# Matmul spacing taken from the trace, in the build-time estimate that orders a two-block network's threads

## The chip, the cores and the metric

The kernel runs on one core of one Trainium2 chip. The metric is the device time of one execution in microseconds (us), the median of several runs.

## The reference, cut to what matters

Two blocks of two layers each, one after the other, in 32-bit floats; the width is 1024.

```
x = first_block(x, c, ctx, ...)          # 256 tokens x and 256 of context, depth 2
    per layer: x += 0.5 * gate * swiglu(norm(x) @ w1) @ w2
               x += gate * mixer(norm(x))     # layer 0 gated delta rule, layer 1 windowed attention
               x += 0.5 * gate * swiglu(norm(x) @ w1) @ w2
return second_block(x, positions, ...)   # 256 tokens, depth 2
    per layer: mix = (x @ w_in -> RG-LRU and latent attention, merged) @ w_out
               x = layer_norm(ALPHA * x + mix)
               ffn = (gelu(conv(x @ w_up)[gate]) * conv(x @ w_up)[value]) @ w_down
               x = layer_norm(ALPHA * x + ffn)
```

The gated delta rule of layer 0 has 8 heads. For each head and both directions it needs the inverses of unit lower triangular matrices of 128 (one for each of four chunks).

## The kernel before, in words

**Dense products.** Each weight piece (128 rows, 1024 or 768 columns) is loaded by SyncE into an `r` tile. `convert` (L464) rounds it to a high part with `copy` (a CAST from `r` to a `w` tile, on ScalarE or VectorE), and `lower` (L482) subtracts to get a low part with `flex` (a TENSOR_TENSOR from `r`, `w` to `w`, on VectorE or GpSimd). `mm3` (L518) then runs three matmuls for each 128 x 128 piece of weights: high with high, high with low, low with high. The moving side has 512 tokens in the first block and 256 in the second. Such matmuls read `p<-b,w` in the trace.

**Small fp32 products.** The mixers use plain 32-bit matmuls (`p<-b,b`); each of these leaves two records in the trace. In the delta rule each head goes through `dn_first` (L1062, grams and decays), `dn_solve` (L1175), `dn_join` (L1214), `dn_inverse` (L1313) and `dn_scan` (L1347). `dn_solve` sends the diagonal blocks of 32 to DRAM (`d<-b`) and back in another layout (`r<-d`), inverts their blocks of 16 in 28 small GpSimd instructions, each in place on the result of the one before, and sends the result back by DRAM (`d<-r`, `b<-d`). `dn_join` puts the blocks together, 16 to 32 to 64 to 128, in six groups of small matmuls (the first is `16*32 16x16`, then 32x16, 32x32, two of 64x64 and so on) with a VectorE or ScalarE step between each two.

**What sets the order.** Nothing is scheduled on the chip: each engine executes its instructions in the order in which the program was built. The build keeps one thread for the main products (priority 9) and spawns threads for everything else: the join has priority 1, the solve 2, grams and scan 3, the tiles of the projection 5. Every call on an engine first goes through `Ker.note` (L278), which adds an estimated duration to that engine's clock and remembers when each tile is written and read. `Ker.run` (L337) takes the first thread in rank whose data are ready when the TensorE clock gets there:

```
r = max([self.wrote[x.tensor.name][0] + 200 for x in aps], default=0.0)
if e:
    r = max(r, self.clock[e] - SLACK)
if best is None or r < best[0]:
    best = (r, th)
if r <= self.clock["tensor"]:
    break
```

The same clocks choose engines: `flex` (L402) takes VectorE or GpSimd, `copy` (L409) ScalarE or VectorE, `affine` (L416) ScalarE or VectorE, each the one that would be through first, counted from the later of its own clock and TensorE's. Their durations are formulas: a copy of n elements is 75 + 0.83 n ns on ScalarE and 65 + 0.52 n on VectorE, a subtraction 65 + 1.04 n on VectorE and 60 + 2.28 n on GpSimd.

In the second block `query_rope` (through `rope`, L1866) turns four tiles of queries per layer, each with one matmul of 256 columns against a constant `b` tile; the stage of w_up (48 pieces per layer, 24 matmuls of 256 columns each) is the longest dense stage. All instructions are issued from one helper, so every row of the trace names line L242 (after the change L260) and is told apart by its tiles: `w` weight parts, `r` raw weights, `b` blocks, `p` PSUM banks, `s` small tiles, `io` and `cbf` constants.

Of the kernel before, what the change touches and what calls it, by code (L numbers as in the profile page):

```python
# [8 lines left out]
F32 = mybir.dt.float32  # L9
F32R = mybir.dt.float32r  # L10
# [6 lines left out]
P = 128  # L17
# [10 lines left out]
# ---------------------------------------------------------------- constants and columns  # L28
# [68 lines left out]
def vec(a):  # L97
    """[..., 128*n] -> [128, prod(...)*n]: a column for each feature tile."""
    import numpy as np

    return np.ascontiguousarray(a.reshape(-1, P).T)
# [16 lines left out]
def pack_w(w):  # L118
    """[K, N] -> [N/128, 128, K]: for an output tile, partition p holds W[k*128+p, 128 columns] for each k."""
# [6 lines left out]
def layouts(a):  # L126
    """The device's arrays from the inputs: layout only."""
# [14 lines left out]
    # the first two slots with the summed features on the partitions, the others with the outputs there  # L142
# [12 lines left out]
    # six tiles of outputs: from the heads that are there early by two, for three tiles, and from each of the others  # L155
# [37 lines left out]
# ---------------------------------------------------------------- order of the work  # L193
# [4 lines left out]
def weave(items, extra):  # L198
    """extra spread evenly among all but the first and the last items, in order."""
# [9 lines left out]
def pieces():  # L209
    """The weights in the order in which they are used: what each product thread pulls next."""  # L210
# [19 lines left out]

class Engine:
    """An engine of the core: each instruction also goes on the estimate of when the engines are busy."""
# [24 lines left out]
class Ker:  # L257
# [19 lines left out]
    # -- the estimate of time, and the threads that it orders  # L277
    def note(self, eng, op, a, k):  # L278
# [7 lines left out]
        if eng == "tensor":  # L286
            if op == "matmul":
                m = aps[2]
                n = math.prod(m.shape[1:])
                c = n * {F32: 1.68, BF16: 0.44}.get(m.dtype, 0.422)  # L290
                if m.dtype == F32 and o.shape[0] <= 64:
                    c *= o.shape[0] / P
            else:
                c = 109.0
# [30 lines left out]
    def need(self, *aps, b=0, p=0, s=0, when=None, e=None):  # L325
        """What a thread waits for: data, free blocks, banks and small tiles, a condition, an engine."""
        return aps, b, p, s, when, e
# [9 lines left out]
    def run(self):  # L337
        """Steps of the threads: the first in rank that can go on when the tensor engine gets there."""
# [20 lines left out]
    # -- memory on chip  # L359
# [1910 lines left out]
```

## Time and profile before

| what | value |
|---|---|
| three runs | 2881.67, 2881.69 (median), 2883.3 us |
| span of the profiled execution | 2879.2 us |
| TensorE (PE) busy | 2760.1 us, 96% |
| VectorE (DVE) busy | 2161.7 us, 75% |
| ScalarE (ACT) busy | 909.9 us, 32% |
| GpSimd (POOL) busy | 672.1 us, 23% |
| chain that ended last | PE 82%, DVE 11%, issue 3%, ACT 2% |

The profiled execution's time is told by its span, 2879.2 us, which lies 2.5 us under the median of the runs; no other time of that execution is shown. The share of the chain says for how much of the span each engine did the work that the end waited for.

### The profile page before, as it was taken

The numbers are of one execution on the slowest core, as the hardware profiler recorded it, in microseconds if no ns is written. First come the engines' busy times: TensorE is split into PE (matmuls) and PEld (weight loads), VectorE is DVE, ScalarE is ACT, GpSimd is POOL, SyncE is SP. The second block draws the span as 40 slices with busy tenths as digits, with TensorE's granted clock in tenths as the row PEclk, the third lists the DMA queues.
The fourth block names the chain that finished last, engine by engine and source line by source line (L and its number), as shares of the span: only waits on it lengthen the run. The fifth ranks groups of instructions, "written<-read, shape, count | busy, mean of one in ns | idle before, by whom it ended". The sixth has DMA issues, their size and how long they took to land.

```text
span 2879.2 us, 47744 instructions
## 1 busy us (share of the span) xinstructions
PE 2760.1 (96%) x18916; PEld 2461.9 (86%) x18916; DVE 2161.7 (75%) x3981; ACT 909.9 (32%) x1979; POOL 672.1 (23%) x678
## 2 busy tenths in 40 slices
PE   7999999999989999999999999999898999999998
PEld 6888888888868888888888877999888998888998
DVE  4788878767766777758866587975878986878995
ACT  2111126435423111021111254214654333753432
POOL 2000234435412000120001322102413322512230
PEclk9999999989999999999999999999999999999999
DMA  6556542212122545535665312655434555334653
GB/s 242 193 181 196 190 162 74 55 43 60 38 96 89 187 151 178 159 109 195 193 202 176 110 62 80 190 179 172 140 110 146 183 176 164 127 110 129 197 174 118
DMA packets 145121, 412.59 MB, mean 143 GB/s; under 512 B 31233, under 2 KB 38145, under 8 KB 144897
## 3 DMA queue, kind: packets, MB, share of 16 engines
q1 hardware_dynamic: 144896, 409.54, 44.9%
q8 instruction: 149, 2.44, 0.4%
q14 instruction: 76, 0.61, 0.1%
HBM read 397.95 MB, written 11.53 MB: 142 GB/s over the span
## 4 chain that ended last, share of the span: by engine, by line
PE 82%; DVE 11%; issue 3%; ACT 2%; POOL 1%; DMA 1%; SPq 0%; POOLq 0%; ACTq 0%; DVEq 0%
PE p L242 82%; DVE b L242 7%; DVE w L242 3%; ACT b L242 2%; DVE s L242 1%; POOL b L242 1%; ACT w L242 1%; POOL w L242 0%; DMA b<-in_ada 0%; DMA b<-in_xt 0%; POOL s L242 0%; ACT L242 0%; DMA b<-d 0%; DVE gs L242 0%; DMA d<-r 0%
## 5 line engine op out<-in xcount | busy, mean ns | idle before, releaser
L242 PE MATMUL p<-b,w 128*128 128x256 f32 (+1 forms) x14166 | 2370.6, 328 | 36.2 <-ACT b L242 13.2
L242 PEld LDWEIGHTS p<-b,w 128*128 128x128 f32 x14166 | 2090.1, 193 | 256.3 <-ACT b L242 17.6
L242 DVE TENSOR_TENSOR w<-r,w 128x1024 fp32r<-128x1024 f32 (+1 forms) x512 | 653.8, 1280 | 54.0 <-ACT w L242 41.6
L242 POOL TENSOR_TENSOR b<-b,b 128x256 fp32r<-128x256 f32 (+3 forms) x262 | 274.6, 1060 | 748.8 <-ACT b L242 559.7
L242 POOL TENSOR_TENSOR w<-r,w 128x1024 fp32r<-128x1024 f32 (+1 forms) x79 | 190.8, 2415 | 1016.3 <-ACT w L242 868.3
L242 DVE CAST w<-r 128x1024 fp32r<-128x1024 f32 (+1 forms) x366 | 262.1, 716 | 184.9 <-PE p L242 153.0
L242 DVE SCALAR_TENSOR_TENSOR b<-r,b 128x512 f32<-128x512 f32 x448 | 343.7, 767 | 11.4
L242 ACT CAST b<-b 128x256 fp32r<-128x256 f32 (+1 forms) x284 | 130.7, 467 | 657.2 <-DVE b L242 571.3
L242 ACT CAST w<-r 128x1024 fp32r<-128x1024 f32 (+1 forms) x225 | 228.4, 1021 | 245.2 <-PE p L242 127.8
L242 PE MATMUL p<-b,b 128*128 128x128 f32 (+8 forms) x2872 | 272.5, 260 | 23.8 <-DVE b L242 15.3
L242 PEld LDWEIGHTS p<-b,b 32*32 32x32 f32 (+4 forms) x2872 | 213.5, 149 | 64.5 <-issue 20.9
L242 DVE TENSOR_TENSOR b<-b,b 128x256 fp32r<-128x256 f32 (+3 forms) x245 | 158.6, 653 | 117.1 <-ACT b L242 112.0
L242 ACT ACTIVATE b<-b 128x256 f32<-128x256 f32 (+1 forms) x188 | 90.8, 495 | 425.3 <-DVE b L242 404.8
L242 ACT ACTIVATE b<-p 128x128 f32<-128x128 f32 (+2 forms) x280 | 114.8, 415 | 293.0 <-PE p L242 292.7
L242 DVE TENSOR_TENSOR b<-b,p 128x256 f32<-128x256 f32 (+1 forms) x234 | 114.9, 501 | 45.7 <-PE p L242 39.5
L242 DVE SCALAR_TENSOR_TENSOR b<-p,par_t,b 128x255 f32<-128x255 f32 (+2 forms) x240 | 106.3, 474 | 16.0 <-ACT b L242 14.8
L242 ACT COPY b<-p 128x512 f32<-128x512 f32 (+5 forms) x161 | 71.7, 458 | 129.6 <-PE p L242 69.1
L242 PE MATMUL p<-io,b 128*128 128x128 f32 (+3 forms) x580 | 88.6, 281 | 19.4 <-DVE b L242 11.8
L242 POOL TENSOR_TENSOR b<-b 128x256 f32<-128x256 f32 x50 | 57.7, 1154 | 175.3 <-DVE b L242 175.3
L242 PEld LDWEIGHTS p<-io,b 128*128 128x128 f32 (+2 forms) x580 | 69.2, 163 | 33.6 <-DVE b L242 10.4
L242 DVE SCALAR_TENSOR_TENSOR b<-p,mod,b 128x256 f32<-128x256 f32 x92 | 40.7, 478 | 71.3 <-PE p L242 71.3
L242 POOL TENSOR_TENSOR s<-s,mhalf 128x4 f32<-128x4 f32 (+2 forms) x36 | 35.6, 990 | 182.5 <-DVE s L242 171.3
(105 smaller groups left out, 1324.1 us busy)
## 6 DMA issues: line engine op xcount, KB each, us to landing
r<-in_w SPq DMA_DIRECT2D x240, 512.0 KB, 3.7
r<-in_ada SPq DMA_DIRECT2D x128, 512.0 KB, 4.2
r<-in_w_up SPq DMA_DIRECT2D x96, 512.0 KB, 3.6
r<-in_w_in SPq DMA_DIRECT2D x76, 512.0 KB, 3.7
r<-in_w_down SPq DMA_DIRECT2D x48, 512.0 KB, 3.6
r<-in_dn_in SPq DMA_DIRECT2D x33, 512.0 KB, 3.6
r<-in_w SPq DMA_DIRECT2D x32, 384.0 KB, 3.3
b<-in_ada SPq DMA_DIRECT2D x32, 256.0 KB, 5.4
```

Of the source, the lines that this page charges most:

```text
L242: return fn(*a, **k)
```

## The change

In `note`, the cost of a TensorE instruction now comes from a function of the weights, the moving tile and the columns, with the numbers that the trace shows for the spacing of such matmuls. Removed comments and docstrings change nothing in the program.

```diff
+PARTS = {(32, 32): 28.0, (16, 32): 29.0, (64, 64): 57.0}
+
+def array_ns(w, x, cols):
+    n, rows = math.prod(x.shape[1:]), w.shape[0]
+    if x.dtype == BF16:
+        return 6.0 + n / 2.4
+    if x.dtype == F32R:
+        return max(112.0, 13.3 + n / 2.4)
+    if (rows, cols) in PARTS:
+        return 2 * PARTS[rows, cols]
+    part = (0.62 if rows <= 64 else 1.0) * (0.25 if cols <= 32 else 0.5 if cols <= 64 else 1.0)
+    return 2 * part * max(110.0, n / 1.2)
...
         if eng == "tensor":
-            if op == "matmul":
-                m = aps[2]
-                n = math.prod(m.shape[1:])
-                c = n * {F32: 1.68, BF16: 0.44}.get(m.dtype, 0.422)
-                if m.dtype == F32 and o.shape[0] <= 64:
-                    c *= o.shape[0] / P
-            else:
-                c = 109.0
+            c = array_ns(aps[1], aps[2], o.shape[0]) if op == "matmul" else 112.0
```

The set of TensorE instructions is the same. In the estimate a dense matmul of 512 columns goes from 216 to 226.6 ns, one of 256 from 108 to 120.0 ns, a block of 32 x 32 from 13.4 to 56 ns, one of 16 columns on 32 rows from 6.7 to 58 (16 rows) or 56 ns, one of 64 x 64 from 53.8 to 114 ns. Over the program the choice of engine moves, from before to after: CAST of 1024 columns to `w` on VectorE 340 to 388, on ScalarE 199 to 151; CAST of 768 columns on VectorE 26 to 30, on ScalarE 26 to 22; low parts of 1024 columns on VectorE 472 to 483, on GpSimd 67 to 56; low parts of 768 on VectorE 40 to 42, on GpSimd 12 to 10; TENSOR_TENSOR `b<-b` of 256 columns on VectorE 8 to 37, on GpSimd 50 to 21.

The delta rule, on PE: the third group of a head's join (32x32) and what follows it up to that head's next small group (64x64, the one that reads b_4218). Before:

```order
MATMUL p_4424<-b_4218,b_4152 32x32 x8
MATMUL p_4425<-b_4152,b_4218 32x32 x16
MATMUL p_4454<-b_3087,w_4104 128x512
...
MATMUL p_4454<-b_3130,w_4104 128x512
MATMUL p_4454<-b_3129,w_4104 128x512
MATMUL p_4480<-b_3146,b_3619 64x64 x4
MATMUL p_4480<-b_3146,b_3667 64x64 x4
MATMUL p_4489<-b_4329 32x16 x32
```

Now, at the like place of a join (its next small group of the same head reads b_4502):

```order
MATMUL p_4657<-b_4502,b_4442 32x32 x8
MATMUL p_4658<-b_4442,b_4502 32x32 x16
MATMUL p_4689<-b_3139,b_3819 64x64 x4
MATMUL p_4689<-b_3139,b_3911 64x64 x4
MATMUL p_4698<-b_4548 32x16 x32
MATMUL p_4732<-b_3145,b_4502 64x64 x4
MATMUL p_4732<-b_3146,b_4502 64x64 x4
MATMUL p_4742<-b_4639,b_4548 32x16 x32
```

The twelve dense matmuls that stood behind the 32x32 groups are gone from there; between the 32x32 and the 64x64 groups of one head now stand only small groups, of this and of another head whose join is under way too (b_4548).

The stage of w_up in layer 0 of the second block, on ACT, in its steady part (`w<-r` is a cast of weights, `p,par_t` and `b<-b` belong to the convolution and the gelu). Before:

```order
ACTIVATE b_20919<-p_20925,par_t 128x256
CAST w_20992<-r_20888 128x1024
ACTIVATE b_20919<-p_20961,par_t 128x256
CAST b_21016<-b_20847 128x256
ACTIVATE b_20919<-b_20919 128x256
ACTIVATE b_20991<-p_20997,par_t 128x256
```

Now:

```order
ACTIVATE b_20708<-p_20748,par_t 128x256
ACTIVATE b_20780<-p_20786,par_t 128x256
CAST b_20849<-b_20708 128x256
ACTIVATE b_20780<-b_20780 128x256
ACTIVATE b_20780<-p_20819,par_t 128x256
ACTIVATE b_20851<-p_20857,par_t 128x256
```

Casts of weights no longer stand between them: of a layer's 48 casts of w_up ScalarE has 8, at the head of the stage, where it had 18, and VectorE 40, where it had 30. The 46 low parts on VectorE and 2 on GpSimd stay; of the TENSOR_TENSOR of 256 columns of that stage some 4 come to VectorE.

The turning of the queries in the same layer, on PE (the matmuls that read b_15401). Before:

```order
MATMUL p_18495<-b_17795,w_18366 128x256 x3
MATMUL p_18512<-b_17638,w_18395 128x256 x3
MATMUL p_18512<-b_17641,w_18395 128x256 x3
MATMUL p_18512<-b_17644,w_18395 128x256 x3
MATMUL p_18512<-b_17647,w_18395 128x256 x3
MATMUL p_18525<-b_18462,b_15401 128x256
MATMUL p_18512<-b_17650,w_18395 128x256 x3
MATMUL p_18512<-b_17653,w_18395 128x256 x3
MATMUL p_18512<-b_17656,w_18395 128x256 x3
MATMUL p_18543<-b_18479,b_15401 128x256
MATMUL p_18552<-b_18493,b_15401 128x256
MATMUL p_18561<-b_18505,b_15401 128x256
```

Now:

```order
MATMUL p_18495<-b_17758,w_18366 128x256 x3
MATMUL p_18502<-b_18464,b_15401 128x256
MATMUL p_18495<-b_17795,w_18366 128x256 x3
MATMUL p_18521<-b_18481,b_15401 128x256
MATMUL p_18530<-b_18493,b_15401 128x256
MATMUL p_18539<-b_18514,b_15401 128x256
MATMUL p_18548<-b_17638,w_18418 128x256 x3
```

The first of the four stands 15 dense matmuls earlier in the work, the last 21, and 3 dense matmuls lie among them where 9 did.

## Rows read from the trace of the kernel before

**Rows 1.** The page: span and busy time of each engine.

```profile
span 2879.2 us, 47744 instructions
...
PE 2760.1 (96%) x18916; PEld 2461.9 (86%) x18916; DVE 2161.7 (75%) x3981; ACT 909.9 (32%) x1979; POOL 672.1 (23%) x678
```

**Rows 2.** Waits of PE over the whole span: total, times, longest.

```profile
PE p L242 <- DVE b L242: 34.0, 35, 3.2
PE p L242 <- ACT b L242: 27.1, 27, 2.3
PE p L242 <- DMA b<-in_ada: 13.0, 1, 13.0
PE p L242 <- DVE w L242: 11.1, 9, 3.2
```

**Rows 3.** Stretches: length, busy PE, PEld, DVE, ACT, POOL, then PEclk, DMA, GB/s.

```profile
72.00:144.00 72.00, 72.00 (x320) 59.61 (x319) 54.77 (x108) 11.49 (x18) 2.58 (x1) 1.00 0.58 193
...
606.30:623.40 17.10, 17.10 (x177) 13.98 (x174) 5.55 (x18) 1.87 (x5) 0.00 (x0) 0.50 0.05 20
...
2206.00:2355.00 149.00, 147.68 (x1217) 146.63 (x1216) 137.97 (x206) 63.68 (x122) 47.12 (x41) 1.00 0.57 177
```

**Rows 4.** Groups of instructions, 2206 to 2355: busy us, mean ns, idle before.

```profile
L242 DVE TENSOR_TENSOR w<-r,w 128x1024 fp32r<-128x1024 f32 x50 | 68.6, 1374 | 2.3 <-ACT w L242 1.2
L242 DVE CAST w<-r 128x1024 fp32r<-128x1024 f32 x35 | 25.7, 733 | 0.2 <-PE p L242 0.2
...
L242 DVE TENSOR_TENSOR b<-b,b 128x256 fp32r<-128x256 f32 x12 | 5.1, 426 | 6.6 <-ACT b L242 6.6
...
L242 ACT CAST w<-r 128x1024 fp32r<-128x1024 f32 x17 | 17.5, 1049 | 8.0 <-PE p L242 8.0
```

**Rows 5.** Groups of instructions over the whole span, by engine.

```profile
L242 DVE TENSOR_TENSOR w<-r,w 128x1024 fp32r<-128x1024 f32 x472 | 612.1, 1300 | 47.9 <-ACT w L242 36.6 <-issue 0.3
...
L242 DVE CAST w<-r 128x1024 fp32r<-128x1024 f32 x340 | 247.0, 726 | 148.2 <-PE p L242 121.7 <-DMA r<-in_w 17.5 <-issue 8.5
...
L242 ACT CAST w<-r 128x1024 fp32r<-128x1024 f32 x199 | 207.0, 1046 | 211.0 <-PE p L242 109.2 <-DMA r<-in_w 79.7 <-issue 14.9
...
L242 POOL TENSOR_TENSOR w<-r,w 128x1024 fp32r<-128x1024 f32 x67 | 168.7, 2518 | 975.4 <-ACT w L242 827.4 <-DVE w L242 78.4 <-DVE b L242 55.0
```

**Rows 6.** Timeline of SyncE: start, us. A solve's first transfer, of heads 3 and 7.

```profile
572.99 0.37 SPq L242 DMA_DIRECT2D d<-b  x1
...
774.48 0.37 SPq L242 DMA_DIRECT2D d<-b  x1
```

**Rows 7.** Timeline of PE in the delta rule: start, us, what ended a wait before.

```profile
604.99 2.15 PE L242 MATMUL p<-b 16*32 16x16 f32 x64 [1.75 <-ACT b L242]
...
611.21 4.18 PE L242 MATMUL p<-b,b 32*32 32x16 f32 x68
...
772.59 2.54 PE L242 MATMUL p<-b,b 32*32 32x16 f32 x68
...
807.52 1.14 PE L242 MATMUL p<-b 16*32 16x16 f32 x35
```

**Rows 8.** Waits of PE from 573 to 606.

```profile
PE p L242 <- ACT b L242: 2.2, 2, 1.7
PE p L242 <- DVE b L242: 1.9, 3, 1.0
```

**Rows 9.** Waits of PE from 774.5 to 807.6.

```profile
PE p L242 <- DVE b L242: 2.0, 1, 2.0
PE p L242 <- POOL b L242: 0.9, 1, 0.9
PE p L242 <- ACT b L242: 0.7, 1, 0.7
```

**Rows 10.** Timeline of PE at the turning of the queries, layer 0.

```profile
2052.11 0.67 PE L242 MATMUL p<-b,b 128*128 128x256 f32 x2 [2.21 <-DVE b L242]
2054.79 1.62 PE L242 MATMUL p<-b,b 128*128 128x256 f32 x3 [2.01 <-DVE b L242]
```

**Rows 11.** Timeline of DVE and POOL at 412.

```profile
412.72 2.37 POOL L242 TENSOR_TENSOR w<-r,w 128x1024 fp32r<-128x1024 f32 x1 [2.81 <-DVE w L242]
412.89 2.48 DVE L242 TENSOR_TENSOR b<-b,b 128x256 fp32r<-128x256 f32 x1
```

## The prediction, made before the changed kernel ran

> **What bounds the kernel now.** I read the page first [rows 1]: TensorE is busy 2760.1 of 2879.2 us, VectorE three quarters of the time, ScalarE and GpSimd a third and less. No product is added or taken away, so TensorE's own work stays, and the change can move three things: the waits of TensorE, the time in which it runs at its lower clock, and, where VectorE is as full as TensorE, the pace of that stage. The view of TensorE's waits [rows 2] then gives the ceiling of a gain from the first: its four largest rows hold 34.0 + 27.1 + 13.0 + 11.1 = 85.2 us, and the 13.0 at the start (the first load of the modulation's weights) is not touched. They are many small ones: 35 waits for a block of VectorE at 1 us each, 27 for one of ScalarE.
>
> The stretches say where there is room. In the first FFN TensorE is busy 72.00 of 72.00 us with VectorE at 54.77 [rows 3]: 320 matmuls at 225 ns each. There any choice of engines is hidden. In the stage of w_up VectorE is at 137.97 of 149 us with TensorE at 147.68 [rows 3]: the tightest place for VectorE. In the delta rule a stretch of 17.1 us has the granted clock at 0.50, the lower level of 1.2 GHz, with TensorE busy all along. The same 68 records of 32x16 take 4.18 us there and 2.54 us where the clock is whole [rows 7], so such a stretch costs 17.1 x (1 - 2.54/4.18) = 6.7 us.
>
> **TensorE's work: 0.** The new estimate's 226.6 ns is nearer to the 225 ns of the row than the old 216, but the chip does the same matmuls.
>
> **The choice of engines.** From counts of the change and durations of rows 4 and 5: VectorE takes 48 casts x 726 ns = 34.8 us, 11 low parts x 1300 ns = 14.3, 29 subtractions or products of 256 columns x 426 ns = 12.4, and a few smaller ones (4 casts and 2 low parts of 768 columns, some 5 us by the rows' price for each column): near 67 us more on an engine that has 2879 - 2162 = 717 us free. ScalarE gives up 48 x 1.05 = 50 us, GpSimd 11 x 2.52 = 28 for the low parts and more for the rest. In all stages of 512 columns TensorE covers this, and it costs nothing; without that cover 67 us would be the bound.
>
> The w_up stage is where it isn't free. VectorE takes 10 casts more a layer x 733 ns = 7.3 us and 4 products x 426 ns = 1.7 [rows 4]: 9.0 us, onto 137.97, which makes 147.0 against 147.7 of TensorE. The ten lie in the steady part, where now every cast is VectorE's: its load for a piece, 138/50 = 2.76 us, grows by about 0.33 x 0.69 + 0.03 = 0.26 us (0.69 is the cast less the overlap of neighbours, an estimate from the busy 137.97 and the sum of its groups, some 147 us in 206 instructions), to 3.02 us, and a piece takes TensorE 24 x 147.68/1217 = 2.91 us. VectorE falls behind by 0.11 us a piece over 40 pieces, 4.4 us, of which a lead of one piece, 2.9 us, can be used up without a wait. I take +2 a layer, **+4** for the two; the ends are 0 (the lead suffices) and +9.0 a layer (VectorE's 11 us of idle time stay where they are).
>
> One row speaks against that. A subtraction of VectorE that takes 0.43 us elsewhere [rows 4] took 2.48 us beside a GpSimd instruction of 2.37 us and ended just after it [rows 11], so work taken from GpSimd can shorten VectorE's too. The Trainium skill states it as a rule ("SBUF — State Buffer", section "Who interferes with whom"): a VectorE instruction with two inputs in SBUF contends with a GpSimd instruction that reads SBUF, and the one that issues second waits out the first. By that rule the +67 would be partly paid back and w_up would cost 0 instead of +4, which makes the sum below 4 us smaller. I keep +4, as in w_up itself the low parts on GpSimd stay at 2 and only some 4 small products leave it.
>
> **The delta rule: +4.** A head's solve is a chain of two trips through DRAM and 28 GpSimd instructions. From its first transfer to the first group of its join there pass 604.99 - 572.99 = 32.0 us for head 3 and 807.52 - 774.48 = 33.0 for head 7 [rows 6, 7]; both had waits of TensorE inside, 2.2 + 1.9 = 4.1 us [rows 8] and 2.0 + 0.9 + 0.7 = 3.6 us [rows 9], so 33 us is about as short as the chain gets. The order says how much TensorE work lies between these two points. I counted it for the eight heads at the spacings of the trace (225 ns for 512 columns, twice 112 for an fp32 matmul of 128, 2.54/34 = 75 ns or less for the smallest). Before: 43.2, 41.2, 44.4, 24.8, 36.2, 37.8, 37.5, 26.1 us. Only heads 3 and 7 lie under 33, by 8.2 and 6.9, 15.1 together; they paid 7.7, half of it. In the new order: 31.6, 34.1, 32.7, 29.0, 27.7, 33.2, 24.1, 29.9 us. The mean falls from 36.4 to 30.3, since a matmul of a join now counts 56 to 114 ns and not 7 to 54, and the planner needs fewer of the others to fill the same estimated time. Six heads lie under 33, by 1.4, 0.3, 4.0, 5.3, 8.9 and 3.1, 23.0 together. Half of that is 11.5; less the 7.7 that go it is **+4**. Ends: -7.7 (every join finds its data) and 23.0 - 7.7 = +15 (every missing microsecond is waited for).
>
> **Inside the joins: 0 for the links, +2 for the clock.** Between two groups of one head there lies less dense work: the twelve dense matmuls of the first excerpt, 2.7 us, are gone. In their place stand 8 of 64x64 and 32 of 32x16, some 3 us of another head by the rows' spacing [rows 7], so that the link is still covered; ends 0 and +4. The longest run of TensorE without a dense matmul grows from about 12 to about 21 us (same spacings). The stretch at 0.50 came right after a wait and a group of 64 small records [rows 3, 7]; a third of one more such stretch, 6.7 / 3, gives **+2** (0 to +6.7).
>
> **Turning the queries: +1.5.** Waits of 2.21 and 2.01 us stand there [rows 10], on VectorE. The first of the four now comes 15 dense matmuls earlier, 15 x 121 ns = 1.8 us, the last 21, 2.5 us. The chain of the four starts 1.8 us sooner but has 2.5 us less dense work in front of its end: 0.7 us a layer more, two layers. Ends: -2 and +5.
>
> **The rest: 0.** Norms and the windowed attention have their steps in nearly the same order, with waits of 1 to 2 us that can go either way; ends -6 and +6 from a dozen of them.
>
> **Sum.** 0 + 4 + 4 + 0 + 2 + 1.5 + 0 = 11.5 us on the span of 2879.2, which gives 2890.7; the runs' median stands 2.5 above that span, so the forecast is **2893.2 us**, slower by 0.4%. A measurement of this kernel can tell about 0.2%, 5.8 us, from no change.
>
> **Rivals.**
> *Faster: the new covers sit better on the chains.* Heads 3 and 7, the two that wait now, get 29.0 and 29.9 us where they had 24.8 and 26.1. If the chain of a solve is also shorter than 33 us because GpSimd has less else to do, their 7.7 us go, and with them the slow stretch that begins right behind head 3's wait, 6.7 us. With nothing lost elsewhere that gives 2881.7 - 14.4 = 2867 us; with half of it 2874. It decides at a chain of 29 us. For it: GpSimd loses low parts of 2.5 us each in the delta rule's projection. Against it: head 6 has only 24.1, head 4 27.7. Chance 0.32, from here down to all that ends under 2875.9.
> *No change.* The joins lose what the tail gains and w_up's lead suffices: the sum without +4 and +4 is 2885; with the rule above it is 2889 and near. From 2875.9 to 2887.5: chance 0.20.
> *Slower still: w_up bound by VectorE.* The change doesn't quite do what it says: one engine's durations come from the trace, the others' do not. The formulas give 597 ns for a cast of VectorE and 1130 for a low part, where the rows have 726 and 1300 [rows 5], and 925 for ScalarE's cast against 1046. Against an exact TensorE the planner thinks VectorE has 15% more room than it has, and gives it all casts. If its idle 11 us don't shrink, w_up costs 9.0 us a layer, and the time is 2893.2 - 4 + 18 = 2907. It decides when TensorE's waits for `w` of VectorE in w_up pass some 3 us a layer. The Trainium skill ("Perfetto Trace Analysis", section "Optimizing Scalar/DVE Operations") says that, if VectorE is saturated, moving some of its work to ScalarE may make sense; this change moves it the other way in that stage. Chance 0.14.
>
> **How the numbers follow.** The forecast's own case, 2887.5 to 2900, has 0.34; with the 0.14 above it, slower has 0.48. Faster has 0.32 and no change 0.20. The low end takes in the faster rival's 2867, the high end w_up bound by VectorE at 2907 and most of the joins' +15 - 4 = 11 on top: 2867 to 2918. The case's own range is 2887 to 2900.
>
> **What would show it.** Right: in the profile after, waits of TensorE in the delta rule from six heads, each 1 to 4 us before a `16*32 16x16` group; VectorE at 146 us or more of a w_up stretch, without a ScalarE cast in its steady part; the dense stretches at 225 ns as before. Wrong: a delta rule that is shorter, with its stretches at 0.50 fewer; or a w_up stage with waits for `w`; or a VectorE total that grows by much less than 67 us, which would mean that GpSimd's share had held it up.

## The result, and the profile after

The changed kernel takes **2927.08 us** (median of 4 runs, 2922.75 to 2929.09) against 2881.68 us before (a fourth run, 2877.81 us, beside the three of the table): a ratio of 1.0161, with a 95% interval of 1.0146 to 1.0176. The direction was forecast, the size wasn't: 1.6% where 0.4% stood, and above the range's end of 2918.

The page of the kernel after, span and busy times:

```profile
span 2924.8 us, 47773 instructions
...
PE 2783.1 (95%) x18916; PEld 2480.1 (85%) x18916; DVE 2204.9 (75%) x4077; ACT 861.0 (29%) x1931; POOL 595.6 (20%) x630
```

The span grew by 45.6 us. TensorE does the same 18916 matmuls and is yet busy for 23.0 us more [rows 1]: it ran longer at the lower clock. The other 22.6 us are idle time. Waits of PE after (total, times, longest):

```profile
PE p L260 <- DVE b L260: 62.9, 53, 4.5
PE p L260 <- ACT b L260: 27.6, 26, 2.3
...
PE p L260 <- DVE w L260: 4.8, 6, 1.1
```

Against [rows 2] the waits for a block of VectorE went from 34.0 to 62.9 us, from 35 to 53 in number; ScalarE's stayed, and those for weights fell by 6.3 us. Where the time lies shows when each stage is cut at the first matmul that reads its weights. The lengths below are worked out so from the trace of the one profiled execution of each kernel (w_down of layer 1 ends with TensorE's last matmul); "waits" sums TensorE's idle times over 0.15 us, "low" the time at the lower of its two clock levels (granted 0.50, 1.2 GHz).

| stage | before: us (waits, low) | after: us (waits, low) |
|---|---|---|
| delta rule, to the second FFN | 477.2 (26.2, 55.7) | 502.0 (38.1, 87.4) |
| windowed attention | 162.0 (14.1, 6.3) | 169.3 (18.6, 20.5) |
| w_down, layer 0 | 80.3 (4.3, 3.4) | 86.1 (7.3, 8.5) |
| w_down, layer 1 | 75.8 (2.7, 0.0) | 81.7 (5.7, 6.8) |
| w_up, each layer | 141.2 | 141.2 |
| all else | 1801.5 | 1803.3 |

So 24.8 us come from the delta rule, 7.3 from the windowed attention, 5.8 and 5.9 from the stretch right behind w_up, 1.8 from the rest. In the delta rule two parts nearly add up to it: 11.9 us more of waits, and 31.7 us more at the lower clock, at 1 - 2.54/4.18 = 0.39 [rows 7] another 12.4, an estimate.

**Inside a join.** Timeline of VectorE and TensorE in the last head's join, kernel after:

```profile
825.50 1.87 PE L260 MATMUL p<-b 16*32 16x16 f32 x64 [0.60 <-issue]
827.30 3.91 PE L260 MATMUL p<-b,w 128*128 128x512 f32 x9
831.24 0.56 DVE L260 CAST w<-r 128x768 fp32r<-128x768 f32 x1 [5.84 <-PE p L260]
831.84 0.96 DVE L260 TENSOR_TENSOR w<-r,w 128x768 fp32r<-128x768 f32 x1
832.71 0.34 DVE L260 TENSOR_SCALAR b<-p,s 128x128 f32<-128x128 f32 x1
833.11 2.25 PE L260 MATMUL p<-b,b 32*32 32x16 f32 x64 [1.91 <-DVE b L260]
```

The first group is through at 827.4. The step that takes its result (TENSOR_SCALAR, 0.34 us) could run then, and comes at 832.71. In front of it in VectorE's queue stands the CAST of an output weight, idle for 5.84 us until TensorE has ended the dense matmuls, and so released a `w` buffer, and a subtraction behind it. The nine dense matmuls that were to cover the step hold up the cast that holds up the step: TensorE waits 1.91 us. The same pattern gives waits of 1.94 and 2.07 us at two later groups of this join. Over the delta rule the waits in front of groups of 32x16, 32x32 and 64x64 went from 0.4 to 7.5 us (summed from the trace); those in front of the first groups (16x16), where a join waits for its solve, from 2.25 to 1.60.

**The solves.** From a solve's first transfer to the first group of its join there pass, for the eight heads, 28.2, 32.3, 42.9, 28.7, 26.1, 34.6, 28.7 and 34.5 us in the kernel after. Five of the eight groups start without a wait, that of head 4 (the fifth of the numbers) among them:

```profile
654.94 0.38 SPq L260 DMA_DIRECT2D d<-b  x1
...
681.06 1.90 PE L260 MATMUL p<-b 16*32 16x16 f32 x64
```

So a solve can be through in 26.1 us, well under the 33 that I had taken for about its least. TensorE's waits between such two points, each counted once, went from 10.0 to 13.1 us in all.

**The clock.** Stretches of the kernel after (columns as in [rows 3]):

```profile
537.40:571.60 34.20, 34.20 (x460) 30.30 (x459) 14.59 (x46) 4.99 (x15) 5.38 (x4) 0.55 0.12 37
554.50:571.60 17.10, 17.10 (x217) 15.99 (x214) 7.53 (x24) 2.06 (x7) 0.00 (x0) 0.50 0.01 2
...
72.00:144.00 72.00, 72.00 (x319) 59.67 (x318) 57.62 (x117) 8.89 (x14) 0.00 (x0) 1.00 0.58 185
```

TensorE is busy for all of them. The first holds the second: the clock fell to 0.50 at 537.4, was whole again for 3.4 us from 551.1, and fell once more at 554.5 for 17.1 us. The second is plain fp32 matmuls, most of them small, of two heads' joins; the third is the dense FFN, still 72/319 = 225.7 ns a matmul, at the full clock. The timeline shows what TensorE did before each fall:

```profile
535.10 1.89 PE L260 MATMUL p<-b 16*32 16x16 f32 x64 [0.82 <-DVE b L260]
...
544.22 2.64 PE L260 MATMUL p<-b,b 128*128 128x128 f32 x36
546.50 4.19 PE L260 MATMUL p<-b,w 128*128 128x512 f32 x9
550.62 2.25 PE L260 MATMUL p<-b,b 32*32 32x32 f32 x64
552.80 1.96 PE L260 MATMUL p<-b 16*32 16x16 f32 x64
554.69 19.52 PE L260 MATMUL p<-b,b 64*64 64x64 f32 x238
```

The first fall came 2.3 us behind a wait of 0.82 us and its group of 64 small records. No wait lies between that and the second fall. Ahead of it come nine dense matmuls at the lower clock, two small groups of different heads without a wait or a dense matmul between them, then 238 records of plain fp32 matmuls (a timeline row takes in all shapes of one kind of tiles: 64x64, 32x16, 32x32 and 128x128), 19.5 us. This is the place of the excerpt from the delta rule in "The change". The link that lost its twelve dense matmuls there costs no wait, but the 17.1 us cost 6.7 by the clock alone.

**Behind w_up.** Waits of PE around the first products of w_down, layer 0, before (2343 to 2378) and after (2375 to 2410):

```profile
PE p L242 <- POOL b L242: 0.7, 1, 0.7
PE p L242 <- DVE b L242: 0.5, 1, 0.5
```

```profile
PE p L260 <- DVE b L260: 1.5, 1, 1.5
PE p L260 <- POOL b L260: 1.5, 1, 1.5
PE p L260 <- ACT b L260: 1.2, 1, 1.2
```

After its first 9 us, with 2.6 us of waits before and after, TensorE is not held up in w_up. But VectorE falls behind. I measured from the end of each piece's matmuls to the end of the first of VectorE's two steps of convolution on it: before, from the 11th piece on, this moves between 4.4 and 6.9 us with no trend; after, it grows from 4.2 us at the 8th piece to 9.2 at the 46th, 0.13 us a piece. It is paid when w_down needs the last product. VectorE's stretch in the middle, before and after:

```profile
2296.00:2331.00 35.00, 35.00 (x294) 35.00 (x293) 32.66 (x49) 13.61 (x27) 11.54 (x10) 1.00 0.60 184
```

```profile
2330.00:2365.00 35.00, 35.00 (x294) 35.00 (x293) 34.48 (x53) 10.40 (x24) 8.18 (x8) 1.00 0.57 171
```

VectorE's 32.66 of 35 us became 34.48, and ScalarE fell from 13.61 to 10.40. In 70 us of the stage VectorE now waits for nothing; before, it waited 4.1 us.

### The profile page after: what moved, and what is told of

The parts are those of the page before. It is cut to its first block, busy times and chain, and to the rows that moved or that the text cites. A ratio compares the mean times of both kernels' runs of the same rounds, so it can differ in the third digit from the quotient of the medians.

```text
span 2924.8 us, 47773 instructions
## 1 busy us (share of the span) xinstructions
PE 2783.1 (95%) x18916; PEld 2480.1 (85%) x18916; DVE 2204.9 (75%) x4077; ACT 861.0 (29%) x1931; POOL 595.6 (20%) x630
## 5 line engine op out<-in xcount | busy, mean ns | idle before, releaser
L260 PE MATMUL p<-b,w 128*128 128x256 f32 (+1 forms) x14166 | 2382.0, 329 | 37.6 <-ACT b L260 16.2
L260 DVE TENSOR_TENSOR w<-r,w 128x1024 fp32r<-128x1024 f32 (+1 forms) x525 | 675.1, 1287 | 39.3 <-ACT w L260 25.3
L260 DVE CAST w<-r 128x1024 fp32r<-128x1024 f32 (+1 forms) x418 | 289.5, 693 | 191.4 <-PE p L260 171.4
L260 POOL TENSOR_TENSOR w<-r,w 128x1024 fp32r<-128x1024 f32 (+1 forms) x66 | 158.9, 2407 | 1014.2 <-ACT w L260 800.0
L260 DVE SCALAR_TENSOR_TENSOR b<-r,b 128x512 f32<-128x512 f32 x448 | 331.6, 740 | 11.3
L260 PE MATMUL p<-b,b 128*128 128x128 f32 (+9 forms) x2872 | 282.0, 267 | 33.5 <-DVE b L260 24.5
L260 PEld LDWEIGHTS p<-b,b 32*32 32x32 f32 (+5 forms) x2872 | 222.3, 155 | 78.0 <-issue 27.7
L260 DVE TENSOR_TENSOR b<-b,b 128x256 f32<-128x256 f32 (+3 forms) x251 | 155.6, 628 | 107.8 <-ACT b L260 103.0
L260 ACT CAST w<-r 128x1024 fp32r<-128x1024 f32 (+1 forms) x173 | 174.9, 1018 | 150.0 <-PE p L260 88.8
L260 DVE SCALAR_TENSOR_TENSOR b<-p,par_t,b 128x254 f32<-128x254 f32 (+2 forms) x240 | 110.9, 477 | 17.2 <-ACT b L260 14.9
L260 POOL TENSOR_TENSOR s<-s,mhalf 128x4 f32<-128x4 f32 (+2 forms) x36 | 34.5, 959 | 247.0 <-DVE s L260 246.9
L260 DVE SCALAR_TENSOR_TENSOR b<-p,cw,b 128x510 f32<-128x510 f32 (+1 forms) x96 | 69.3, 739 | 2.2 <-ACT b L260 1.8
```

Source lines behind the costliest of these rows:

```text
L260: return fn(*a, **k)
```

## The experiments

Eighteen more kernels ran. The table has the same stages for all, from one profiled execution each; "time" is the median of the runs, with the ratio to the runs of the kernel before on the same chip. (The expectations below were written with the stages cut some 50 us later in the second block and in the delta rule: what they call w_up, 140 and 146 us, reaches into w_down, and their delta rule, 529 and 553, into the second FFN; 486 and 512 are a shorter cut of it. The differences between kernels are nearly the same; for the windowed attention it is 10 us there, 171 and 181, and 7.3 here.)

| kernel | time | ratio, 95% | delta rule (waits, low) | windowed att. | w_down 0 |
|---|---|---|---|---|---|
| before | 2881.7 | | 477.2 (26.2, 55.7) | 162.0 | 80.3 |
| after | 2927.1 | 1.0161, 1.0146 to 1.0176 | 502.0 (38.1, 87.4) | 169.3 | 86.1 |
| e1_dense_only | 2912.2 | 1.0112, 1.0032 to 1.0192 | 487.9 (33.3, 69.1) | 166.2 | 85.4 |
| e2_fp32_only | 2887.8 | 1.0034, 1.0009 to 1.0058 | 489.4 (29.0, 82.6) | 157.0 | 80.0 |
| e3_order_new_choice_old | 2900.6 | 1.0061, 1.0041 to 1.0080 | 492.8 (26.1, 99.7) | 163.5 | 80.2 |
| e4_order_old_choice_new | 3217.3 | 1.1171, 1.1089 to 1.1254 | 502.8 (35.3, 89.4) | 161.0 | 89.3 |
| e5_wup_casts_back | 2913.0 | 1.0142, 1.0064 to 1.0220 | 496.7 (39.0, 72.3) | 166.7 | 84.4 |
| e6_all_engines_traced | 2908.7 | 1.0127, 1.0051 to 1.0203 | 486.5 (33.6, 65.8) | 164.0 | 80.8 |
| e7_dense_2pct | 2904.4 | 1.0112, 1.0035 to 1.0189 | 503.6 (37.6, 85.5) | 162.4 | 79.7 |
| e8_fp32_2pct | 2901.8 | 1.0103, 1.0026 to 1.0180 | 487.5 (32.9, 61.4) | 168.5 | 80.2 |
| e9_wup_wdown_back | 2924.0 | 1.0157, 1.0124 to 1.0191 | 503.8 (38.6, 89.4) | 166.6 | 86.4 |
| e10_old_up_to_delta | 2896.5 | 1.0068, 1.0049 to 1.0087 | 462.3 (25.2, 23.9) | 166.6 | 86.1 |
| e11_fp32_from_window | 2871.2 | 0.9985, 0.9969 to 1.0001 | 474.6 (26.4, 47.8) | 157.0 | 80.0 |
| e12_dense_tenth_pct | 2904.6 | 1.0090, 1.0058 to 1.0122 | 501.9 (39.9, 81.9) | 163.2 | 80.2 |
| e13_hold_w_down | 2945.8 | 1.0238, 1.0188 to 1.0289 | 506.3 (36.2, 99.3) | 168.6 | 90.4 |
| e14_dn_oe_off_vector | 2920.5 | 1.0151, 1.0101 to 1.0200 | 498.8 (35.6, 85.7) | 169.1 | 86.0 |
| e15_e11_dn_oe_off_vector | 2877.6 | 1.0005, 0.9988 to 1.0022 | 470.8 (28.3, 41.0) | 157.0 | 80.2 |
| e16_change_tenth_pct | 2910.7 | 1.0117, 1.0051 to 1.0183 | 499.4 (30.0, 102.4) | 168.8 | 85.5 |
| e17_dn_out_off_vector | 2912.6 | 1.0123, 1.0082 to 1.0163 | 490.3 (32.9, 76.8) | 165.9 | 85.7 |
| e18_fp32_from_window_again | 2873.6 | 0.9986, 0.9968 to 1.0004 | 477.2 (26.1, 55.7) | 157.1 | 80.2 |

### Which part of the change, and by which way

`array_old` is the old formula. First the two halves of the new costs alone.

```diff
# e1_dense_only
-            c = array_ns(...)
+            c = (array_old if aps[2].dtype == F32 else array_ns)(...)
# e2_fp32_only
+            c = (array_ns if aps[2].dtype == F32 else array_old)(...)
```

> The new spacing only for the dense matmuls (and bf16 and transposes), the old formula for plain fp32 matmuls. In the w_up stages the choice of engines is exactly that of the changed kernel (VectorE 40 casts a layer, ScalarE 8), so all theories expect both stages at 146 us against 140 before, +12 us. Theory A (it is VectorE's load, which the dense spacing moves): the delta rule's stages (dn_in and dn_oe, 486 us before, 512 after) and the windowed attention's (171 before, 181 after) are long too, some +30 us in all: about 2920 us. Theory B (it is the order of the small matmuls, which the fp32 costs move): delta rule and windowed attention as before: about 2894 us. Theory C (the delta rule's order is sensitive to any change of the estimate): its length moves, by no rule.

> The new costs only for plain fp32 matmuls, the old ones for the dense ones. In the w_up stages casts and low parts are chosen exactly as before the change: 140 us each. Theory A: delta rule and windowed attention near 486 and 171 us: about 2882 us. Theory B: they stay long, 512 and 181: about 2917 us. Theory C: the delta rule's length moves, by no rule.

Behind w_up the answer is clean: 85.4 us with the dense spacing alone, 80.0 with the fp32 costs alone. It is the dense spacing that sends the casts there to VectorE. In the delta rule neither A nor B holds: each half alone lengthens it, by 10.7 and 12.2 us, which leaves C, a length that moves by no rule.

Then two estimates side by side, one for the order of the threads and one for the choice of engines.

```diff
# e3: order by the new costs, engines by the old; e4: the reverse
     def note(self, eng, op, a, k):
+        for m, f in ((1, array_old), (0, array_ns)):
+            self.clock, self.wrote, self.read = self.times[m]
+            self.note1(eng, op, a, k, f)
...
     def flex(self, n):
-        now = self.clock["tensor"]
+        now = self.chooser["tensor"]
```

> Two estimates are kept: the new one orders the threads, the old one chooses engines. VectorE has only 20 casts a layer in w_up and 34 low parts (GpSimd 14). Theory A: w_up at 140 us or less, the delta rule back toward 486: 2880 to 2890 us. Theory B: w_up at 140, the delta rule and the windowed attention long: about 2915 us. Theory C: the delta rule at some other length.

> The reverse: the old estimate orders the threads, the new one chooses engines (VectorE 38 casts a layer in w_up, 22 casts and 28 low parts in the delta rule's projection, where before had 11 and 22). Theory A: w_up at 145, the delta rule long, 510 or more: 2910 to 2930 us. Theory B: w_up at 145, the delta rule near 486: about 2892 us. Theory C: the delta rule at some other length.

With VectorE relieved (e3) the stretch behind w_up is back at 80.2, and VectorE's lag stays near 5 us through the stage. The delta rule is not: 492.8 us with exactly the waits of before (26.1 and 26.2), all of its 15.6 us in the clock (44.0 us more at the lower level, times 0.39 is 17). So in this profile the order costs by the clock alone; the runs, 1.0061 of before, bear out the size. e4 tells little of the change: where the two estimates part, each cast of w_up comes only just ahead of its use, and w_up takes 287 us. Its delta rule is long as well.

### Small shifts of the estimate

```diff
# e6_all_engines_traced: the other engines' durations from the trace too
-            c = 75 + 0.83 * n + ...           # ScalarE
+            c = 190 + 0.835 * n + ...
-            c = 65 + n * (... 0.52 if fast else 1.04) + ...   # VectorE
+            c = 65 + 0.65 * n + ... if fast else 140 + 1.13 * n + ...
-            c = 60 + n * 2.28                 # GpSimd, tensor_tensor
+            c = 190 + 1.8 * n if n <= 128 else 480 + 1.95 * n
# e7_dense_2pct, e12_dense_tenth_pct: the kernel before with
-                c = n * {F32: 1.68, BF16: 0.44}.get(m.dtype, 0.422)
+                c = n * {F32: 1.68, BF16: 0.44}.get(m.dtype, 0.430)     # e12: 0.4225
# e8_fp32_2pct: the kernel before with F32: 1.72
# e16_change_tenth_pct: the changed kernel with
-        return max(112.0, 13.3 + n / 2.4)
+        return max(112.0, 13.5 + n / 2.4)
```

> The changed kernel, with the durations of VectorE, ScalarE and GpSimd taken from the trace too (a cast of 1024 columns 731, 1045 ns, a low part 1297, GpSimd's 2477). It gives VectorE 19 casts a layer in w_up. If the estimate went wrong because TensorE alone was made true: w_up at 140 us, the delta rule (529 us before, 553 with the change, up to the second FFN) back to 530 or less, the windowed attention at 171: 2880 us or less. If the delta rule is long because of the order that the fp32 costs give, or is sensitive to any change: w_up 140, delta rule 540 to 555: 2895 to 2915.

> The kernel before, with 0.430 instead of 0.422 ns a column for the dense matmuls in the estimate: 2 percent, a seventh of what the change does at 256 columns. If the delta rule follows the size of the cost (load of VectorE, cover of the chains): within 4 us of 529, in all 2880 to 2886. If its order is sensitive to any change of the estimate, and that of before is a lucky or a tuned one: 540 us or more: 2893 or more.

> The kernel before, with 1.72 instead of 1.68 ns a column for the plain fp32 matmuls: 2.4 percent, where the change makes the small ones 2 to 9 times as dear. By size: delta rule within 4 us of 529, in all 2880 to 2886. If sensitive to anything: 540 us or more: 2893 or more.

> The kernel before, with 0.4225 instead of 0.422 ns a column for dense matmuls: a tenth of a percent, too little to mean anything for a load or a cover. If the delta rule's time follows the size of a cost: 529 us within 2, 2882 in all. If the order before is one that happens to fall well: 538 to 555 us there, 2890 to 2908.

> The changed kernel with 13.5 instead of 13.3 ns in the cost of a dense matmul, a tenth of a percent at 512 columns. If the delta rule's 553 us come from the new costs as such: 553 within 5. If they are one case of many: somewhere between 530 and 560, off by more than 5. The w_up stages, whose choices are the same, 146 us each in both cases.

These runs show of what kind the delta rule's 24.8 us are. A tenth of a percent on one constant of the kernel before (e12) makes it 501.9 us, 24.7 more, and the whole kernel 0.9% slower; two percent 503.6 (dense) and 487.5 (fp32); durations from the trace for all engines 486.5. (That estimate, e6, is the nearest to the trace, and yet the kernel is slower than before, also in the second block's mixers: 235.1 and 231.9 us where before had 225.4 and 226.7.) On the changed kernel a tenth of a percent leaves the length nearly the same, 499.4 us (e16), within the 5 us that I had named for "the new costs as such"; but it has 8.1 us less of waits and 15 us more of low clock (30.0 and 102.4 against 38.1 and 87.4). One stretch is 41 us:

```profile
536.40:577.40 41.00, 41.00 (x484) 37.09 (x483) 18.34 (x55) 5.57 (x16) 2.33 (x4) 0.50 0.12 34
```

One order profiled again varies as well: that of before gave 477.2, 474.6 (e11), 477.2 (e18) and, but for its last rows, 462.3 (e10, below), that of the change 502.0, 496.7 (e5), 503.8 (e9) and 506.3 (e13). The two sets lie 19.5 us apart at the least, so these lengths belong to the order, and a tenth of a percent can decide which order comes out. Every one of the eight other orders tried (e1 to e3, e6 to e8, e12, e16; e4 is left out) is longer than the 477.2 of before, by 9 to 26 us. One order varies by up to 15 us, so the four of 9 to 12 us (e1, e2, e6, e8) are weak evidence one by one, and e16 can't tell its two cases apart; e7 and e12 are clear of it. The new costs made the delta rule no longer than those two shifts did. And the order of before beats all eight, so a shift of any kind was likely to lose; whether that order was found by tuning or fell well by chance, nothing here shows.

```diff
# e10_old_up_to_delta: the old costs until the second FFN's first weights come
+            if self.at < self.order.index(("w1", 0, 1, 0)):
+                c = array_old(...)
```

> The old costs up to the end of the delta rule, the new ones from there. Up to the last rows of the delta rule its order is that of the kernel before. If the order made there is the cause of the delta rule's 24 us: 529 us there (525 to 533), the rest as with the change, near 181 for the windowed attention and 146 for each w_up: 2900 us. If something outside the order does it: 550 and 2925.

With the old order back, but for its last rows, the delta rule is short (462.3, with even less low clock), while the rest stays as with the change: 166.6 and 86.1. The whole kernel falls to 1.0068 of before (1.0049 to 1.0087) from the change's 1.0161, clear of the spread: it is the order made there, with its choice of engines, that costs the delta rule its time.

### Behind w_up

```diff
# e5_wup_casts_back; e9_wup_wdown_back also has DOWN, a table for w_down
-            self.copy(h[:, :n], t[:, :n])
+            (self.nc.scalar.copy if UP[at] == "A" else self.nc.vector.tensor_copy)(h[:, :n], t[:, :n])
# e13_hold_w_down
+            if j == 22:
+                self.most = 2
...
+                if (k, m) == (0, 2):
+                    self.most = NHL
```

> The changed kernel, but in w_up each cast of weights goes to the engine that had it before (ScalarE 18 a layer, VectorE 30). All that comes ahead of w_up is as in the changed kernel. If VectorE's casts are what makes w_up long: both stages at 140 us (146 with the change), without the low clock at their end: 2927 - 12 = 2915 us. If it is something else there (the other choices, the order): 146 us and 2927.

> The changed kernel, with the casts of w_up and of w_down each on the engine that had them before (in w_down VectorE 11 a layer, where the change gives it 17). With w_up alone put back the stage took 144 and 145 us. If the waits at the end of w_up come from casts of w_down that stand ahead of the last product in VectorE's order: both stages at 140 us, without the low clock there: some 9 to 12 us less than the changed kernel, 2915. If the order of the other work does it: 144 to 146 again.

> The changed kernel, but from the 23rd of 24 steps of w_up on at most two converted pieces of weights are kept ready (four else) until the third piece of w_down has been used. TensorE's order is row for row that of the changed kernel; VectorE's casts and low parts of w_down's first pieces stand later in its queue. If they stand ahead of the last products of w_up and make them late: w_up at 140 to 142 us a layer instead of 146, in all 2917. If VectorE's load in the stage does it: 146 and 2927.

Putting the casts back was a miss: 84.4 and 86.4 us. VectorE's load is back (33 of 35 us in the second quarter of w_up, as before), but its lag grows all the same, in e9 from 4.7 to 9.0 us. Waits of VectorE in 70 us of w_up, e9 and then e6 (before has 4.1 us for products there, none for weights):

```profile
DVE w L264 <- ACT w L264: 3.0, 2, 1.5
```

```profile
DVE w L260 <- ACT w L260: 7.9, 12, 0.8
```

In e9 VectorE waits for casts that ScalarE brings late. But that alone does not explain the lag: in e6 it waits longer for such casts, and there, as in e3, the lag doesn't grow. In those two the planner itself left VectorE with 30 to 32 us of 35. So in before, after, e3, e5, e6 and e9 a lag that grows goes with a long stretch behind w_up; why the casts put back by hand did not end it stays open.

e13 moves w_down's weights behind w_up's last products in VectorE's queue, with TensorE's order unchanged. Waits of PE there:

```profile
PE p L260 <- DVE w L260: 11.7, 4, 6.9
PE p L260 <- DVE b L260: 0.5, 1, 0.5
```

The three waits for the last products are gone, as the queue's theory has it, but w_up and w_down now wait 11.7 us for weights: 146.5 and 90.4 us, the slowest of the variants but e4. It seems that VectorE has no room there, so that what it does first decides only which wait it is.

### Casts ahead of a join's steps

```diff
# e14_dn_oe_off_vector; e17_dn_out_off_vector: if key[0] in ("dn_oe", "dn_ol")
+            if key[0] == "dn_oe":
+                self.nc.scalar.copy(h[:, :n], t[:, :n])
+                self.lower()
+                self.nc.gpsimd.tensor_tensor(lo[:, :n], t[:, :n], f(h[:, :n]), ALU.subtract)
+                self.free(t)
```

> The changed kernel, with the six pieces of the delta rule's output weights that come ahead of the last head's join cast by ScalarE and their low parts taken by GpSimd, so that VectorE has neither in its queue there. The order up to the last head is that of the changed kernel. If casts and low parts that stand ahead of a join's own steps on VectorE make the last join late (three waits of 1.9, 1.9 and 2.1 us inside it, and the low clock of 17 us between 834 and 862): these waits go and most of that low clock, the delta rule 553 - 6 - 6 = 541 us, in all 2915. If the join's own chain is too long for what covers it: waits of the same size and 550 or more.

> As the run with the six pieces taken from VectorE, and the two pieces that follow them too. There the wait between the first two groups of the last head's join stayed at 1.91 us, with the cast of the seventh piece in front of the step in VectorE's queue. If a cast that waits for TensorE to release its buffer, standing ahead of the join's step, is what makes that wait: it goes (under 0.6 us), the waits from the first group of that join on fall from 7.4 us by 2 or more, the delta rule 545 us, in all 2915. If the step is late for another reason: 1.9 us again.

With six pieces off VectorE (e14) the wait of 1.94 us went, that of 2.07 fell to 0.61, and that of 1.91 stayed, for the seventh piece's cast now had its place:

```profile
834.38 3.86 PE L260 MATMUL p<-b,w 128*128 128x512 f32 x9
838.28 0.56 DVE L260 CAST w<-r 128x768 fp32r<-128x768 f32 x1 [5.80 <-PE p L260]
838.87 0.96 DVE L260 TENSOR_TENSOR w<-r,w 128x768 fp32r<-128x768 f32 x1
839.75 0.34 DVE L260 TENSOR_SCALAR b<-p,s 128x128 f32<-128x128 f32 x1
...
840.15 2.04 PE L260 MATMUL p<-b,b 32*32 32x16 f32 x63 [1.91 <-DVE b L260]
```

Nothing was gained: the three waits fell by 3.4 us together, but 2.33 us stand in front of that join's first group (0.60 with the change) and 2.52 behind the join (0.41). The delta rule's 498.8 us lie within what the change's order shows from run to run, and the forecast of 12 us less failed.

With eight off (e17) the step follows its matmuls at once, and all three waits inside that join are gone (waits of PE from 820 to 870: 7.4 us in e14, 5.4 here; what is left stands in front of the join's first group and behind the join):

```profile
828.41 1.87 PE L260 MATMUL p<-b 16*32 16x16 f32 x64 [1.51 <-DVE b L260]
830.20 2.34 PE L260 MATMUL p<-b,w 128*128 128x512 f32 x9
830.31 0.35 DVE L260 TENSOR_SCALAR b<-p,s 128x128 f32<-128x128 f32 x1 [2.00 <-PE p L260]
...
832.48 1.89 PE L260 MATMUL p<-b,b 32*32 32x16 f32 x64
832.63 0.83 ACT L260 CAST w<-r 128x768 fp32r<-128x768 f32 x1 [6.85 <-PE p L260]
833.54 1.83 POOL L260 TENSOR_TENSOR w<-r,w 128x768 fp32r<-128x768 f32 x1 [5.86 <-ACT w L260]
```

The dense matmuls between take 2.34 us here, not 3.9: the clock held too. The delta rule falls to 490.3 us, 11.7 less than with the change, from 5.2 us of waits and 10.6 of low clock (times 0.39 is 4.1; the rest lies within what one order shows from run to run). Against the four profiles of the change's order it is 6.4 to 16.0 us less. The whole kernel's 1.0123 (1.0082 to 1.0163) is not clear of the change's 1.0161. So the cast in front of the step is shown as the cause of these three waits, and they are one part of the 24.8 us; how large a part is not shown more closely than this.

### The new fp32 costs from the windowed attention on

```diff
# e11_fp32_from_window, e18 (the same): the old costs, but from the windowed attention on
+            if aps[2].dtype == F32 and op == "matmul" and self.at >= (place of the first "swa_qk"):
+                c = array_ns(...)
# e15: the same, with the edit of e14
```

> The kernel before, with the new costs for plain fp32 matmuls from the windowed attention on: the one place where a part of the change was shorter (167 us against 171 in the run of that part alone). The delta rule stays as before. If that gain belongs to the costs: 167 there, 2877 us, a ratio near 0.9985. If it was another case of an order that falls one way or the other: 170 to 180, 2880 to 2890.

> The kernel before with the new fp32 costs from the windowed attention on, once more, for a narrower interval. If its 4 us in the windowed attention are real: a ratio of 0.9985 within 0.001; if the first comparison was scatter: 1.000.

> The kernel before with the new fp32 costs from the windowed attention on, and the same six pieces on ScalarE and GpSimd. If VectorE's queue costs the last head's join something there too (2.0 us of wait at its start): 2 to 5 us less than without, near 2868, a ratio of 0.995 to 0.9975. If it is only another order: anything from there to 2885.

The windowed attention takes 157.0 or 157.1 us in e2, e11, e15 and e18 against 162.0 before: 5 us that repeat. The whole time is 0.9985 and 0.9986, with intervals that just reach 1. The version is faster than the changed kernel; that it is faster than the one before is likely, not shown. e15, with the edit of e14 on top, came to 1.0005: no gain, the second case of what was expected of it.

## Why the prediction was right or wrong

The direction was right. Of the 45.6 us the delta rule took 24.8 where the terms 4, 0 and 2 stood, w_up 11.7 where 4 stood, the windowed attention 7.3 where 0 stood, and all the rest 1.8.

**Right:** TensorE's work stayed (225.7 ns a dense matmul, the FFN's stages within 1 us of before). ScalarE gave up 48.9 us where 50 stood. The turning of the queries: I had +0.7 us a layer for it; its waits went from 4.2 to 6.9 us in layer 0 (1.08, 4.48 and 1.36), but a wait of 2.59 us for weights behind it went, and the layer's mixer is 0.8 and 0.5 us longer.

**The load of VectorE: paid back in part.** It grew by 43.2 us, not 67. Its rows after:

```profile
L260 DVE TENSOR_TENSOR w<-r,w 128x1024 fp32r<-128x1024 f32 x483 | 632.2, 1310 | 36.0 <-ACT w L260 23.3
L260 DVE SCALAR_TENSOR_TENSOR b<-r,b 128x512 f32<-128x512 f32 x448 | 331.6, 740 | 11.3
L260 DVE CAST w<-r 128x1024 fp32r<-128x1024 f32 x388 | 272.6, 703 | 143.2 <-PE p L260 126.5 <-DMA r<-in_w 11.7 <-issue 3.6
```

The second of them was, before:

```profile
L242 DVE SCALAR_TENSOR_TENSOR b<-r,b 128x512 f32<-128x512 f32 x448 | 343.7, 767 | 11.4
```

A cast fell from 726 to 703 ns [rows 5] and this SCALAR_TENSOR_TENSOR, the same 448, from 767 to 740, 12.1 us in all; a low part did not (1300 to 1310), while GpSimd lost 76.5 us. The rule of the Trainium skill ("SBUF — State Buffer", section "Who interferes with whom") speaks of VectorE instructions with two inputs in SBUF. The traces agree: of the 448, which have two, those that overlap a GpSimd instruction in time take 1498 ns on average and the others 690, and of the first kind there are 43 before and 32 after. The low parts, which have two as well, take 1503 ns beside GpSimd and 1223 else, but here the first kind hardly got rarer (130 and 120). That w_up would cost nothing did not follow.

**w_up: the mechanism right, the term too small.** I had VectorE falling behind by 0.11 us a piece for 40 pieces; it is 0.13. The failed step is "a lead of one piece can be used up without a wait", +2 us a layer. The lag is paid behind the stage: 3.0 us of waits a layer and, for which I had no term there, 5.1 to 6.8 us more at the lower clock, 5.8 and 5.9 us together. The rival "w_up bound by VectorE" had 9.0, and its test, waits for `w` in w_up, was wrong: the wait is for the last products, behind the stage.

**The delta rule: the wrong steps.** "33 us is about as short as the chain gets" was wrong: head 7's first group had no wait in front of it [rows 7], so its 33.0 us was a bound from above, and after, one chain is through in 26.1 us. So "half of what the cover lacks is waited for", +4, priced something that seldom holds a join up. All waits between the two points grew by some 3 us, near the +4, but that is luck: only 1.60 us of them stand in front of a first group, less than the 2.25 before. The rival "faster" had its condition in four chains, under 29 us, and its gain did not come: the 17.1 us of low clock behind head 3's first group became 6.8, but more came elsewhere, 55.7 to 87.4 us in all. "0 for the links" failed by 7 us. It held at the link of the excerpt, and failed in the last head's join, where dense matmuls do stand behind the groups: I asked of such cover only how long it lasts, not what stands ahead of the link's step in VectorE's queue. "+2 for the clock" had the sign and a sixth of the size: 31.7 us more at the lower level, 12.4 us. (The 68 records by which I priced that level are 64 of 32x16 and 4 of 128x128, in both rows, so the ratio stands.) Beneath these lies the larger error: I argued from the size of costs (36.4 to 30.3 us of cover) where a tenth of a percent did as much (e12). No rival had that, though the forecast could have: the order differs over the whole stage, and nothing in a mean of covers says how the pieces of an order fall.

**The windowed attention: "the rest 0".** It cost 7.3 us, 4.5 of waits and 14.2 us of low clock, beyond the ends of 6 that I gave to all of the rest. What in its order does it was not tried; the spread over the runs, 157.0 to 169.3 us, suggests that it is of the same kind.

## What to carry to other kernels

Where an estimate at build time orders the work of several engines, a better constant can be no more than a new draw of the order: judge a change of it by several slightly shifted estimates, not by one, and shift the old estimate too, since its order may be an unusually good one. Dense work covers a small step only if nothing in the other engine's queue ahead of that step waits for the same dense work to end; look at the row ahead of the late instruction. And an engine that falls behind by a tenth of a microsecond a piece may show no wait until the stage ends, so measure its lag along the stage.

## What the runs showed that I had not expected

Of what the change added to the delta rule, TensorE's clock took about as much as its waits (12.4 and 11.9 us), and not only behind waits: 17.1 us (after) and 41.0 us (e16) at 0.50 with TensorE busy throughout, mostly on plain fp32 matmuls. With the order unchanged the delta rule's time at the lower level still differed from profile to profile: 72.3 to 99.3 us with the change's order (waits 36.2 to 39.0), 23.9 to 55.7 with that of before (waits 25.2 to 26.4). What makes it differ was not found.
